# Attention of a two-layer fp32 trunk in 24 sections of fixed TensorE order, its value sums divided in place of its weights, with a 512-wide output product

## The chip, the cores and the metric

The kernel runs on one core of one Trainium2 chip. The metric is device time in microseconds of one execution, taken as the median of several runs. TensorE (PE in the profile), VectorE (DVE), ScalarE (ACT), GpSimd (POOL) and SyncE (SP, which here issues DMAs) each take their own instructions in a fixed order and wait for each other by semaphores.

## The reference

Two layers on 640 tokens of width 1024: one block of 128 context tokens (`xp`) and four of 128 latent tokens (`xs`), all in fp32. Layer 0 has grouped-query attention (8 heads of 64, 2 key heads) beside a depthwise convolution of 31 taps on 512 channels; both go into one output product. Layer 1 is an mLSTM. Each layer ends with a squared-ReLU feed-forward part, and every sub-layer is modulated by vectors from a conditioning product (`_adaln`), six vectors of 1024 a layer.

```python
m = jax.nn.silu(cond) @ w + b          # six modulation vectors a layer
h = x * (1 + scale) + shift
q, k, v, u = jnp.split(h @ w_in, [...])
s = jnp.einsum('bqkgd,bskd->bkgqs', q_r, k_all) * scale   # context: 128 keys; latent: 640 keys
p = jax.nn.softmax(s, axis=-1)
att = jnp.einsum('bkgqs,bskd->bqkgd', p, v_all)
u = a * jax.nn.sigmoid(gt)
u = jax.nn.silu(_layernorm(_depthwise_conv(u, conv_w, conv_b), cln_g, cln_b))
out = jnp.concatenate([att, u], axis=-1) @ w_out          # (640 x 1024) @ (1024 x 1024)
x = _layernorm(ALPHA * x + gate * out, g, b)
x = _layernorm(ALPHA * x + gate2 * (relu(modulate(x) @ w1) ** 2 @ w2), g2, b2)
```

## The kernel before, in words

Large products are made of fp32 numbers split into a rounded high part and a low rest; `mm3` (lines 192 to 195) issues three matmuls for one: high by high, high by low, low by high. Weights come by DMA into a `raw` tile, ScalarE casts the high part `whi` (L166) and GpSimd subtracts the low part `wlo` (L167), both into a ring of slots (`split_piece`).

The program is written in one order, and a scheduler places each instruction in its engine's queue by priorities and estimated times. On the chip each queue then runs as it stands.

Attention (line 1118 on) works on four pairs of heads. `prep(i)` makes the q of a pair: for each token block a cast (L1135) and a subtraction on DVE (L1136) give high and low part, two transposes (L1139) and a copy (L1141) bring them to PE's layout. `weights_of` makes scores with matmuls (L1172 for context, L1186 for a latent block and head, 640 keys) and calls `softmax`: maximum on DVE (L1151), exponential on ScalarE (L1153, it also gives the row sum), reciprocal on DVE (L1154), and the division of the whole row of weights on DVE (L1156, 128 x 640). `values_of` turns the weights with transposes (L1218), copies them out of PSUM (L1221 on ScalarE for key block 0, L1223 on DVE for the others), and multiplies by the values (L1225), key block by key block, into `po`. `put_att` splits the sums into `act_h` and `act_l` (L1160, L1161).

The modulation vectors come from `ada_steps` (L259): the 1024 x 1024 part of `w_ada` is streamed in eight k-tiles (two DMAs of 256 KB each, L287, into slots of the weight ring) and multiplied with 32 columns of the array at a time (L293). `background(n)` issues one such step of each waiting vector; seven vectors are computed during the attention.

`conv(i)` sums the 31 taps of channel block i in one tile `cy`, in one chain: some taps on DVE (L955, L964), the others as a product on ScalarE (L969, tile `tap`, two buffers) and an add on GpSimd (L971). `CONV_DVE` says which taps go to DVE. `conv_norm` (L1254 to L1294) makes the layer norm and the swish; it is called after the ninth of twelve units of the attention.

`out_proj` (L455) makes the 640 x 1024 output product in four groups of 256 columns, each with eight k-tiles at once (0 to 3 attention channels, 4 to 7 conv channels) for the five token blocks; `add_gated` multiplies by the gate and adds to the residual, and `finish` starts the layer norm of a token block. The feed-forward part of layer 0 follows.

## Time and profile before

| | before |
|---|---|
| median of 3 runs | 1731.96 us (1729.14 to 1732.87) |
| profiled execution | 1730.38 us |
| its span, first to last instruction | 1728.4 us |
| mean granted clock of TensorE | 0.971 |
| PE busy | 1603.1 us (93%) |
| DVE busy | 1098.2 us (64%) |
| POOL busy | 1005.0 us (58%) |
| ACT busy | 797.0 us (46%) |
| moved by DMA | 211.76 MB, 123 GB/s |

Busy time is the union of an engine's instructions. PE's matmuls overlap in the records: a duration is longer than the distance from one start to the next, so the pace of PE is read from starts. A fp32 matmul (a modulation step, a value block) leaves two records, a matmul of split parts one. In the rows below, "idle before" is the time an engine stood still ahead of an instruction, and the name after the arrow is what ended it.

### The profile page before, as it was taken

The numbers are of one execution on the slowest core, as the hardware profiler recorded it, in microseconds if no ns is written. First come the engines' busy times: TensorE is split into PE (matmuls) and PEld (weight loads), VectorE is DVE, ScalarE is ACT, GpSimd is POOL, SyncE is SP. The second block draws the span as 40 slices with busy tenths as digits, with TensorE's granted clock in tenths as the row PEclk, the third lists the DMA queues.
The fourth block names the chain that finished last, engine by engine and source line by source line (L and its number), as shares of the span: only waits on it lengthen the run. The fifth ranks groups of instructions, "written<-read, shape, count | busy, mean of one in ns | idle before, by whom it ended". The sixth has DMA issues, their size and how long they took to land. (4 is left out here: it accounts for less than half of the span.)

```text
span 1728.4 us, 27385 instructions
## 1 busy us (share of the span) xinstructions
PE 1603.1 (93%) x10155; PEld 1408.6 (81%) x10155; DVE 1098.2 (64%) x1924; ACT 797.0 (46%) x1560; POOL 1005.0 (58%) x760
## 2 busy tenths in 40 slices
PE   7988899998989999999898998997989999999996
PEld 4678555897879889897798998896988989989885
DVE  2899997669434354356777787688497254344367
ACT  2224676345444444444544555555265444344344
POOL 2245574147956556457655766756459755546555
PEclk9999899998989999999999999998999999999998
DMA  8852785223433223125232222326442422213241
GB/s 302 250 192 82 256 310 189 62 93 122 135 91 98 70 78 98 60 87 185 90 109 81 88 66 93 113 83 201 117 159 79 128 93 92 94 53 98 86 152 68
DMA packets 151309, 211.76 MB, mean 123 GB/s; under 512 B 11845, under 2 KB 92969, under 8 KB 151176
## 3 DMA queue, kind: packets, MB, share of 16 engines
q1 hardware_dynamic: 150944, 209.94, 37.8%
q8 instruction: 80, 1.31, 0.3%
q14 instruction: 53, 0.43, 0.1%
q10 hardware_dynamic: 232, 0.08, 0.0%
HBM read 186.74 MB, written 23.24 MB: 121 GB/s over the span
## 5 line engine op out<-in xcount | busy, mean ns | idle before, releaser
L167 POOL TENSOR_TENSOR wlo<-raw,whi 128x512 fp32r<-128x512 f32 x370 | 512.8, 1408 | 405.6 <-ACT whi L166 391.5
L166 ACT CAST whi<-raw 128x512 fp32r<-128x512 f32 x364 | 222.4, 620 | 427.6 <-PE ps L195 194.3
L193 PE MATMUL ps<-whi,h 128*128 128x512 f32 x640 | 254.4, 399 | 13.7 <-DVE pr L526 6.9
L194 PE MATMUL ps<-wlo,h 128*128 128x512 f32 x640 | 254.8, 398 | 0.0
L195 PE MATMUL ps<-whi,h 128*128 128x512 f32 x640 | 254.3, 397 | 0.0
L193 PE MATMUL ps<-act_h,whi 128*128 128x320 f32 (+2 forms) x704 | 221.9, 317 | 7.2 <-ACT act_h L625 5.9
L194 PE MATMUL ps<-act_l,whi 128*128 128x320 f32 (+2 forms) x704 | 221.6, 315 | 4.2 <-POOL act_l L626 2.2
L195 PE MATMUL ps<-act_h,wlo 128*128 128x320 f32 (+2 forms) x704 | 221.0, 315 | 2.3 <-POOL wlo L167 2.3
L167 POOL TENSOR_TENSOR wlo<-s,whi 128x512 fp32r<-128x512 f32 x118 | 162.8, 1383 | 73.8 <-ACT whi L166 61.3
L758 DVE TENSOR_TENSOR acc<-acc,ps 128x512 f32<-128x512 f32 x120 | 81.9, 685 | 161.6 <-PE ps L195 161.6
L193 PEld LDWEIGHTS ps<-whi,h 128*128 128x128 f32 x640 | 121.7, 190 | 42.8 <-DVE pr L526 7.1
L193 PEld LDWEIGHTS ps<-act_h,whi 128*128 128x128 f32 x704 | 135.7, 193 | 12.3 <-ACT act_h L625 6.7
L195 PEld LDWEIGHTS ps<-whi,h 128*128 128x128 f32 x640 | 121.4, 190 | 29.2
L194 PEld LDWEIGHTS ps<-wlo,h 128*128 128x128 f32 x640 | 121.6, 190 | 27.3
L194 PEld LDWEIGHTS ps<-act_l,whi 128*128 128x128 f32 x704 | 135.6, 193 | 7.3 <-DVE act_l L626 2.8
L195 PEld LDWEIGHTS ps<-act_h,wlo 128*128 128x128 f32 x704 | 135.6, 193 | 3.1 <-POOL wlo L167 3.1
L193 PE MATMUL ps<-whi,act_h 128*128 128x256 f32 x440 | 125.7, 289 | 1.1 <-DVE acc L1094 1.1
L194 PE MATMUL ps<-wlo,act_h 128*128 128x256 f32 x440 | 124.4, 286 | 0.0
L195 PE MATMUL ps<-whi,act_l 128*128 128x256 f32 x440 | 123.3, 286 | 0.0
L971 POOL TENSOR_TENSOR cy<-cy,tap 128x655 f32<-128x655 f32 x50 | 80.4, 1607 | 53.8 <-DVE cy L964 22.5
L193 PE MATMUL ps<-T_h,whi 128*128 128x320 f32 x336 | 104.0, 310 | 4.0 <-ACT pr L550 2.8
L166 ACT CAST whi<-s 128x512 fp32r<-128x512 f32 x120 | 73.2, 616 | 68.9 <-DVE s L501 52.6
(440 smaller groups left out, 4064.1 us busy)
## 6 DMA issues: line engine op xcount, KB each, us to landing
raw<-in_w_ff_dram SPq DMA_DIRECT2D x128, 512.0 KB
whi<-in_w_ada_dram SPq DMA_DIRECT2D x80, 256.0 KB
wlo<-in_w_ada_dram SPq DMA_DIRECT2D x80, 256.0 KB
raw<-in_w_in_m_dram SPq DMA_DIRECT2D x32, 512.0 KB
ada_w<-in_w_ada_dram SPq DMA_DIRECT2D x32, 256.0 KB
acc_d<-acc SPq DMA_DIRECT2D x15, 512.0 KB
raw<-in_w_in_a_dram SPq DMA_DIRECT2D x12, 512.0 KB
rx<-acc_d SPq DMA_DIRECT2D x20, 256.0 KB
```

What stands on the lines that cost most here:

```text
L166: nc.scalar.copy(out=hv, in_=src)
L167: (eng or nc.gpsimd).tensor_tensor(out=lv, in0=src, in1=f32(hv), op=ALU.subtract)
L193: nc.tensor.matmul(out=out, lhsT=lh, rhs=rh, start=start, stop=False)
L194: nc.tensor.matmul(out=out, lhsT=lh, rhs=rl, start=False, stop=False)
L195: nc.tensor.matmul(out=out, lhsT=ll, rhs=rh, start=False, stop=stop)
L758: nc.vector.tensor_tensor(out=x, in0=x, in1=ps, op=ALU.add)
L971: nc.gpsimd.tensor_tensor(out=y, in0=y, in1=tp, op=ALU.add)
```

## The change

- The conv's last channel block takes every third tap on DVE (11) in place of every eighth (4).
- While the attention is written, each PE instruction is tied to the one before it (`in_turn`), so that PE's order is the written one.
- The attention is written as 24 sections, three for each half of a pair of heads: two key blocks turned and copied, scores of later blocks between them, one call for modulation (two k-tiles, `ada_group = 2`, in the first 20 sections), then the values of both blocks; the third section has one key block and the context block or the divisors.
- `prep` makes one cast and one subtraction for all five token blocks (128 x 640 each), and yields between its transposes.
- Weights of latent blocks stay undivided. The row sums of a pair's eight blocks stand in one tile; their reciprocals are spread to 128 x 512, turned by four transposes, and the value sums are multiplied by them (`latent_out`). Context weights are divided on ScalarE.
- Key block 4 instead of block 0 is copied by ScalarE.
- Five modulation vectors instead of seven are computed in the attention; the last two go to the feed-forward part of layer 0.
- x is loaded again and scaled before the last three sections, and `conv_norm` is written after the attention.
- `out_proj_halves` takes 512 columns at a time. The first half runs over the five token blocks twice: k-tiles 0 to 3 (attention), then 4 to 7 (conv), in five PSUM banks. Four of the second half's weight pieces use other tiles than the ring.

```diff
-CONV_DVE = (range(31), range(31), range(0, 31, 4), range(0, 31, 8))
-PT_ACT = (0,)
+CONV_DVE = (range(31), range(31), range(0, 31, 4), range(0, 31, 3))
+PT_ACT = (4,)
-ADA_IN_ATT = 7
+ADA_IN_ATT = 5
+ADA_PAIRS = 20
+    def in_turn(ins):
+        if K.ordered:
+            if K.pe is not None:
+                tc.add_manual_dep(
+                    ins, K.pe.name, mybir.DependencyInfo(mybir.DependencyClass.NoSync, mybir.DependencyReason.DATA),
+                    reason="order of the attention")
+            K.pe = ins
...
-            if k:
+            if k and k % K.ada_group == 0:
                 yield
...
+    def out_proj_halves(w, S, finish):
+        ah, al = act
+        ws = load_n512(w, 0)
+        pss = [ps1() for _ in range(NT)]
+        for k0 in (0, 4):
+            for t in range(NT):
+                sl = slice(t * P, (t + 1) * P)
+                for k in range(k0, k0 + 4):
+                    mm3(pss[t], ah[:, k, sl], al[:, k, sl], *ws[k], k == 0, k == KT - 1)
+                if k0:
+                    add_gated(pss[t], t, S.gate, 0, 512, S.tmp)
...
+        for t in range(NT):
+            ps = ps1()
+            tm_tile(ws, act, t, ps)
+            add_gated(ps, t, S.gate, 512, 512, S.tmp, nc.vector)
+            finish(t)
...
+            qs = att.tile([P, NT, 2, P], F32R, name="qs", bufs=1)
+            nc.scalar.copy(out=qs[:, :, :, 0:64], in_=q)
+            nc.vector.tensor_tensor(out=qs[:, :, :, 64:128], in0=q, in1=f32(qs[:, :, :, 0:64]), op=ALU.subtract)
...
-            nc.vector.reciprocal(out=ri, in_=sm)
-            d2 = dst.rearrange("p a b -> p (a b)") if multi else dst
-            nc.vector.tensor_scalar(out=d2, in0=d2, scalar1=ri[:, 0:1], scalar2=None, op0=ALU.mult)
...
+        def divisors(i):
+            ri = att.tile([P, 8], F32, name="ri8")
+            nc.vector.reciprocal(out=ri, in_=sums[i])
+            rb = rawp.tile([P, 1024], F32, name="raw")
+            nc.vector.tensor_copy(
+                out=rb[:, 0:512].rearrange("p (o d) -> p o d", d=HD), in_=ri.unsqueeze(2).broadcast_to([P, 8, HD]))
+            return rb
+        def divisors_turned(rb):
+            tp = ps1()
+            for t in range(4):
+                transpose(out=tp[:, t * P:(t + 1) * P], in_=rb[:, t * P:(t + 1) * P], identity=ident)
+            nc.scalar.copy(out=rb[:, 512:1024], in_=tp)
+        def latent_out(i, rb):
+            x, sl = rb[:, 512:1024], slice(P, TOK)
+            nc.vector.tensor_tensor(out=x, in0=POs[i], in1=x, op=ALU.mult)
+            nc.scalar.copy(out=act[0][:, i, sl], in_=x)
+            nc.vector.tensor_tensor(out=act[1][:, i, sl], in0=x, in1=f32(act[0][:, i, sl]), op=ALU.subtract)
...
+                p0 = turned(i, s, 0)
+                next_weights()
+                p1 = turned(i, s, 1)
+                if s == 0:
+                    next(parts, None)
+                elif i + 1 < pairs:
+                    context_weights(i + 1)
+                modulation()
+                values(i, s, 0, p0)
+                values(i, s, 1, p1)
...
-        out_proj(I["w_out_a"][0], S, S.finish_mixer("f0"))
+        out_proj_halves(I["w_out_a"][0], S, S.finish_mixer("f0"))
```

The first place is DVE's queue in the middle of the attention. `cy` is the chain of conv taps, `ptok` a row of weights, `nm` a maximum, `ri` a reciprocal. Before:

```order
L1136 TENSOR_TENSOR qs<-acc,qs 128x2x64
L1156 TENSOR_SCALAR ptok<-ptok,ri 128x640
L1151 TENSOR_REDUCE nm<-ps_2779 128x1
L1136 TENSOR_TENSOR qs<-acc,qs 128x2x64
L964 SCALAR_TENSOR_TENSOR cy<-up,cw,cy 128x655
L1154 RECIPROCAL ri<-sm 128x1
L1156 TENSOR_SCALAR ptok<-ptok,ri 128x640
L1151 TENSOR_REDUCE nm<-ps_2910 128x1
```

Now, in the seventh and eighth section (L1251 is the copy of turned weights, L1016 the tap, L1203 the maximum):

```order
L1016 SCALAR_TENSOR_TENSOR cy<-up,cw,cy 128x655
L1251 COPY pT<-ps_2565 128x512
L1016 SCALAR_TENSOR_TENSOR cy<-up,cw,cy 128x655
L1203 TENSOR_REDUCE nm<-ps_2572 128x1
L1251 COPY pT<-ps_2581 128x512
L1285 RECIPROCAL ri_2787<-sums 128x8
L1287 COPY raw<-ri_2787 128x512
L1185 TENSOR_TENSOR qs<-acc,qs 128x10x64
L1203 TENSOR_REDUCE nm<-ps_2631 128x1
L1016 SCALAR_TENSOR_TENSOR cy<-up,cw,cy 128x655
L1203 TENSOR_REDUCE nm<-ps_2640 128x1
```

The divisions of `ptok` and their reciprocals are gone, the five subtractions of q are one, and taps of the conv chain stand between the copies and maxima of neighbouring sections.

The second place is PE's queue in the attention, between the turning of one pair of key blocks and the next (`psc` is a sum of modulation steps, `po` the value sums). Before:

```order
L1218 MATMUL ps1_2445<-ident_75,ptok_2299 128x128
L293 MATMUL psc_2512<-wlo_2562,stat_109 32x256 x2
L1186 MATMUL ps2_2582<-kTA_503,qT_2223 128x320
L1186 MATMUL ps2_2582<-kTB_504,qT_2223 128x320
L293 MATMUL psc_2512<-whi_2631,stat_109 32x256 x2
L293 MATMUL psc_2512<-wlo_2632,stat_109 32x256 x2
L1225 MATMUL po_2307<-pT_2349,vS_505 64x256 x2
L1218 MATMUL ps1_2454<-ident_75,ptok_2260 128x128
```

Now, the end of a third section and the start of the next:

```order
L127 MATMUL ps2_2456<-kTA_503,qT_2112 128x320
L127 MATMUL ps2_2456<-kTB_504,qT_2112 128x320
L127 MATMUL psc_2362<-whi_2465,stat_109 32x256 x2
L127 MATMUL psc_2362<-wlo_2466,stat_109 32x256 x2
L127 MATMUL psc_2362<-whi_2473,stat_109 32x256 x2
L127 MATMUL psc_2362<-wlo_2474,stat_109 32x256 x2
L127 MATMUL po_2184<-pT_2435,vS_505 64x256 x2
L130 MATMUL ps1_2486<-ident_75,ptok_2260 128x128
```

Half k-tiles that stood among scores have become a run of two whole k-tiles, straight ahead of the values.

The third place is PE's queue in the feed-forward part, where a group of first products (`act_h`, 320 wide) and of second products (`h`, 512 wide) meet. Before:

```order
L195 MATMUL ps_5045<-act_h,wlo 128x320
L193 MATMUL ps_5088<-whi,h 128x512
L194 MATMUL ps_5088<-wlo,h 128x512
L195 MATMUL ps_5088<-whi,h 128x512
```

Now, at one such meeting:

```order
L214 MATMUL ps_4602<-wlo,h 128x512
L215 MATMUL ps_4602<-whi,h 128x512
L127 MATMUL psc<-whi,stat 32x256 x2
L127 MATMUL psc<-wlo,stat 32x256 x2
L213 MATMUL ps_4677<-act_h,whi 128x320
L214 MATMUL ps_4677<-act_l,whi 128x320
L215 MATMUL ps_4677<-act_h,wlo 128x320
```

The k-tiles of the two moved vectors stand in seven groups of one to three between the products.

## Rows read from the trace of the kernel before

**Rows 1.** The page's engine line: busy us, share of the span, instructions.

```profile
PE 1603.1 (93%) x10155; PEld 1408.6 (81%) x10155; DVE 1098.2 (64%) x1924; ACT 797.0 (46%) x1560; POOL 1005.0 (58%) x760
```

**Rows 2.** Stretches: length, busy of PE, PEld, DVE, ACT, POOL, clock, DMA share, GB/s.

```profile
183.00:326.00 143.00, 132.28 (x1012) 76.23 (x1009) 123.07 (x254) 86.96 (x181) 68.39 (x48) 0.95 0.62 215
...
240.00:260.00 20.00, 18.96 (x173) 10.31 (x169) 18.59 (x40) 15.02 (x33) 13.37 (x10) 1.00 1.01 373
...
498.00:505.00 7.00, 0.12 (x2) 0.10 (x1) 1.76 (x3) 2.25 (x4) 3.58 (x3) 0.65 0.48 167
540.00:800.00 260.00, 260.00 (x1430) 233.66 (x1429) 116.39 (x181) 110.20 (x180) 146.50 (x111) 1.00 0.28 88
```

**Rows 3.** Timeline of PE: start us, us, engine, line, operation, tiles, count.

```profile
180.62 0.39 PE L293 MATMUL psc<-whi,stat 128*32 128x256 f32 x2
...
182.56 0.39 PE L293 MATMUL psc<-whi,stat 128*32 128x256 f32 x2
...
217.43 0.66 PE L1218 MATMUL ps<-ident,ptok 128*128 128x128 f32 x4
...
218.02 0.41 PE L293 MATMUL psc<-whi,stat 128*32 128x256 f32 x2
...
218.59 0.41 PE L1186 MATMUL ps<-kTA,qT 128*128 128x320 f32 x1
...
224.93 0.65 PE L1225 MATMUL po<-pT,vS 128*64 128x256 f32 x4
225.51 0.66 PE L1218 MATMUL ps<-ident,ptok 128*128 128x128 f32 x4
225.93 0.39 PE L1186 MATMUL ps<-kTA,qT 128*128 128x320 f32 x1
...
226.68 0.44 PE L1225 MATMUL po<-pT,vS 128*64 128x256 f32 x2
...
445.23 0.39 PE L193 MATMUL ps<-whi,h 128*128 128x512 f32 x1
...
459.15 0.31 PE L193 MATMUL ps<-act_h,whi 128*128 128x320 f32 x1
```

**Rows 4.** DVE's groups by shape, 183 to 327 us: busy, mean ns, idle before.

```profile
L1156 DVE TENSOR_SCALAR ptok<-ptok,ri 128x640 f32<-128x640 f32 x32 | 28.7, 896 | 0.5
...
L1136 DVE TENSOR_TENSOR qs<-acc,qs 128x128 fp32r<-128x128 f32 x18 | 10.5, 586 | 0.0
...
L964 DVE SCALAR_TENSOR_TENSOR cy<-up,cw,cy 128x655 f32<-128x655 f32 x6 | 5.3, 890 | 0.0
L1156 DVE TENSOR_SCALAR pp<-pp,ri 128x128 f32<-128x128 f32 x8 | 5.3, 662 | 0.1
```

**Rows 5.** Timeline of DVE: a division of weights.

```profile
212.19 1.91 DVE L1156 TENSOR_SCALAR ptok<-ptok,ri 128x640 f32<-128x640 f32 x1
```

**Rows 6.** Timeline of POOL: two taps of the conv.

```profile
212.17 1.58 POOL L971 TENSOR_TENSOR cy<-cy,tap 128x655 f32<-128x655 f32 x1 [1.52 <-ACT tap L969]
...
267.74 1.57 POOL L971 TENSOR_TENSOR cy<-cy,tap 128x655 f32<-128x655 f32 x1 [0.18 <-ACT tap L969]
```

**Rows 7.** POOL's groups by shape, 132 to 327 us.

```profile
L971 POOL TENSOR_TENSOR cy<-cy,tap 128x655 f32<-128x655 f32 x50 | 80.4, 1607 | 53.8 <-DVE cy L964 22.5 <-ACT tap L969 10.3 <-DVE ri L1154 8.7
```

**Rows 8.** PE's groups by shape, 183 to 327 us: half of the modulation steps.

```profile
L293 PE MATMUL psc<-wlo,stat 128*32 128x256 f32 x203 | 31.7, 412 | 0.0
```

**Rows 9.** ACT's groups by shape, 183 to 327 us.

```profile
L969 ACT ACTIVATE tap<-up,cw 128x655 f32<-128x655 f32 x33 | 27.6, 840 | 13.1 <-POOL cy L971 13.1
```

**Rows 10.** PE's groups by shape, 326 to 386 us: the output product.

```profile
L193 PE MATMUL ps<-whi,act_h 128*128 128x256 f32 x160 | 44.7, 284 | 0.0
```

**Rows 11.** PE's groups by shape, 445.2 to 459.2 us: 512 columns.

```profile
L194 PE MATMUL ps<-wlo,h 128*128 128x512 f32 x20 | 7.9, 395 | 0.0
```

**Rows 12.** Timeline of PE behind the output product.

```profile
407.51 1.01 PE L193 MATMUL ps<-act_h,whi 128*128 128x384 f32 x2 [5.00 <-ACT act_h L625]
```

**Rows 13.** Waits, 480 to 520 us: us in total, times, longest.

```profile
ACT whi L166 <- DMA raw<-in_w_ff_dram: 14.4, 3, 12.4
```

More of the change, by code (lines that the diff above doesn't have):

```diff
@@ new lines, in context_weights @@
+        def context_weights(i):
+            qT, g = qTs[i], i // 2
+            sp = ps2()
+            pp = Ps[i, -1] = att.tile([P, 2, P], F32, name="pp")
+            for h in range(2):
+                for x, kT in enumerate((kTA, kTB)):
+                    matmul(
+                        out=sp[:, h, 0:P], lhsT=qT[:, h, 0:P], rhs=kT[:, g, 0:P], start=(x == 0), stop=(x == 1))
+            for h in range(2):
+                sm = att.tile([P, 1], F32, name="smc")
+                exps(sp[:, h, 0:P], pp[:, h, :], sm, False)
+                ri = att.tile([P, 1], F32, name="ri")
+                nc.vector.reciprocal(out=ri, in_=sm)
+                nc.scalar.activation(out=pp[:, h, :], in_=pp[:, h, :], func=AF.Copy, scale=ri[:, 0:1])
@@ new lines, in turned @@
+        def turned(i, s, j):
+            tp = ps1()
+            for h in range(2):
+                for t in range(2):
+                    o = (h * 2 + t) * P
+                    transpose(
+                        out=tp[:, o:o + P], in_=Ps[i, 1 + 2 * s + t, h][:, j * P:(j + 1) * P], identity=ident)
+            pT = att.tile([P, DEC], F32, name="pT", bufs=2)
+            if j in PT_ACT:
+                nc.scalar.copy(out=pT, in_=tp)
+            else:
+                nc.vector.tensor_copy(out=pT, in_=tp)
+            return pT
@@ new lines, in context_values @@
+        def context_values(i, pT):
+            vg = slice((i // 2) * HD, (i // 2 + 1) * HD)
+            po = ps1()
+            for h in range(2):
+                matmul(
+                    out=po[64 * h:64 * h + 64, 0:P], lhsT=vS[:, 0, vg], rhs=pT[:, h * P:(h + 1) * P],
+                    start=True, stop=True, tile_position=(0, 64 * h))
+            nc.scalar.copy(out=act[0][:, i, 0:P], in_=po[:, 0:P])
+            nc.vector.tensor_tensor(
+                out=act[1][:, i, 0:P], in0=po[:, 0:P], in1=f32(act[0][:, i, 0:P]), op=ALU.subtract)
@@ new lines, in trunk_kernel, with next_weights, modulation @@
+        K.ordered = True
+        pairs = HEADS // 2
+        jobs = [(i, t, h) for i in range(pairs) for t in range(1, NT) for h in range(2)]
+        def next_weights(n=1):
+            for _ in range(n):
+                if jobs:
+                    latent_weights(*jobs.pop(0))
+        section = 0
+        def modulation():
+            nonlocal section
+            if section < ADA_PAIRS:
+                background(1)
+            section += 1
+        for _ in prep(0):
+            pass
```

209 lines of the change are left out of this document (107 added, 102 removed).

## The prediction

> **What bounds the kernel now.** I read the page's engine line first, then busy time by stretches, then the groups of the attention, and last the timeline of TensorE (PE), which gives the spacing of instructions that their durations don't. Of the profiled span of 1728.4 us PE is busy for 1603.1, 93% [rows 1]. So in each stage the question is whether the change leaves PE less to issue, or lets it wait less. The attention runs from 183 to 326 us; VectorE (DVE) is busy for 123 of these 143 us and PE for 132; in the middle, 240 to 260, DVE has 18.6 and PE 19.0 of 20 [rows 2]. So neither can be emptied there without the other setting the pace. The feed-forward part is PE alone, 260.0 of 260 us from 540 to 800 [rows 2], and so is the output product (326 to 386). What is taken from DVE in the attention is worth something; what is added to PE in the feed-forward part costs its full length.
>
> In the timeline I read from one start to the next [rows 3]. Four transposes take 0.42 us when scores follow (225.51 to 225.93) and 0.59 when narrow matmuls of 32 columns of the array follow (217.43 to 218.02): a change of form costs about 0.15. One k-tile of a modulation vector (eight records) on its own takes 0.57 (218.02 to 218.59), in an unbroken run 0.43 (180.62 to 182.56 is nine half k-tiles of 0.215). Four scores with the change are 0.75 (225.93 to 226.68), so 0.60 without. One value block is 0.58 (224.93 to 225.51).
>
> **The change, part by part.**
>
> *Work taken off DVE in the attention.* The 32 divisions of weights are 28.7 us, those of the context weights 5.3 [rows 4]; 40 reciprocals shrink to 12. Larger and fewer subtractions of q (some 7 us less of the 10.5 of L1136) stand against 7 more taps of 0.89 (6.2) and four products of a divisor with a value sum (0.68 each, as the copies of that size). DVE loses about 33 of its 123 us. One division takes 1.91 us where a GpSimd tap has just started (212.17 and 212.19 [rows 5, 6]), against a mean of 0.90; so part of the mean is waiting for GpSimd, and I count the whole of it as gone. By the Trainium skill, SBUF — State Buffer (SBUF: two separate sides), DVE and GpSimd hold one port pair in turn and the loser blocks for a whole instruction; so GpSimd's adds should shorten too when the divisions go. The rows leave little for that: an add takes 1.57 or 1.58 here and 1.61 in the mean [rows 6, 7].
>
> *PE in the attention.* Seven vectors become five, in 20 sections of two k-tiles. Two k-tiles in a run are 2 x 0.43 + 0.15 = 1.0, so 20 us; before, the 405 records in this stretch, half of them in [rows 8], stood in pieces, many of half a k-tile, and summed over the pieces' spacing they take 39 us, with 4 of waiting. Value blocks in pairs: 0.43 + 0.43 + 0.15 = 1.0 for two, against 1.16. Four transposes of divisors for each of four head pairs are new (0.6 each, 2.3 in all). A section with two blocks is then 0.42 + 0.60 + 0.59 + 0.45 (q transposes or context scores) + 1.0 + 1.0 = 4.06, the third of a half about 3.9. The last 16 sections come to 5.33 x 12.0 = 64, less four without a modulation pair (4), six without a score group (4) and about 2 where no q transposes are left, plus the PE work of the conv's norm (10.7 us, summed from the spacing of its records), which the order puts among them: about 65. All 24 by the same count: 98.
>
> *The wait that takes the divisions' place.* The conv's last channel block now has a DVE tap at every third place. Each interval is two GpSimd adds of 1.61 [rows 7], one DVE tap of 0.89 [rows 4] and two handovers, 0.26 together (an estimate from the shortest wait shown for a tap, 0.18 [rows 6]): 4.35. Ten such DVE taps stand in DVE's order between the copies of sections one to eight, so the copies behind each wait for the chain, and PE, itself in fixed order, for the copies. Before, the first weight transposes started at 209; I leave the start at 208, since the q preparation ahead of it still waits for the rotated q. Nine intervals are 39 us: section nine starts at 247, where PE alone would be at 241. ScalarE's taps also stand ahead of exponentials in its queue; it waited 13.1 us for GpSimd in this way [rows 9], and DVE's wait covers that.
>
> So the attention ends at 247 + 65 + 2 (small waits, an estimate from the releasers of its idle time, each under 1 us) = 314 instead of 326: **minus 12**. Bounds: minus 20 (PE alone: 208 + 98) and 0 (the chain gives back everything).
>
> *Output product.* 480 matmuls of 256 columns become 240 of 512. The durations, 283 and 395 ns [rows 10, 11], would shrink the product by 30 per cent, 17 us. The spacing says otherwise: 480 in 57.4 us (60 less the other work of 326 to 386) is 0.120 each; sixty of 512 columns take 445.23 to 459.15, 0.232 each [rows 3]. So 57.4 becomes 55.7. The conv's channels come second, so PE starts without them, but the norm is now last in program order: I add 2 to 3 us of waiting at the second pass (none to 5). The last token tile's layer norm, behind which PE waits 5.0 [rows 12], no longer has weight casts among its work on DVE: minus 2 (0 to minus 4). Sum **minus 1** (minus 6 to plus 4). The Trainium skill, TensorE: Matmul & The Clock Gate (Back-to-back issue gap), gives N/2.4 + 2.5 ns for an isolated matmul, near the rows at both widths, but 131 ns as the sustained figure at 512 columns. By that figure 240 would be an estimated 31 us, 24 below my term; the measured 0.232 is against it.
>
> *Two vectors moved to the feed-forward part.* 16 k-tiles in seven groups between its matmuls, with two changes of form each: 16 x 0.43 + 14 x 0.15 = **plus 9**. Bounds: 18 if every half k-tile costs the 0.57 of a whole one alone [rows 3]; 2 if most of them fill the 6.9 us hole at 498 to 505 [rows 2], where PE waits for weights that arrive late (ScalarE waits 14.4 us for the transfers [rows 13]). Into SP's queue just there go 32 loads of 256 KB more, past the feed-forward weights, so I expect no filling, rather up to 4 us more; I take 9. The same 8 MB leave the attention, where the transfers were once at their ceiling (share 1.01 from 240 to 260 [rows 2]); since PE had 18.96 there, that gives at most 1 us, inside the bounds.
>
> The pool closed early, and x reloaded before the last three sections, are hidden by those sections; late, x would hold only the residual. Nothing.
>
> Sum: -12 - 1 + 9 = -4, on the profiled execution's own 1730.4: 1726.4. That lies 1.6 below the median of the runs (1731.96), which would make it 1728; I give 1727.5. A measurement of this kernel can tell about 0.2% (3.5 us) from no change, so the forecast is just inside faster.
>
> **Rivals.**
>
> 1. *The chain doesn't bind.* GpSimd, with no divisions beside it, adds at 1.57, DVE takes each tap on time, and PE runs from 208 to 306. For it: DVE is left with 90 us of work in 118. Against: ten taps at fixed places. Attention minus 20, total minus 12: 1719.
> 2. *Slower: a ring holds the attention, and the moved vectors are paid in full.* In sections one to eight each DVE tap waits for two GpSimd adds, these for ScalarE's taps, these for the exponentials ahead of them, these for scores, which in PE's fixed order stand behind matmuls that wait for the copies behind the DVE tap. It decides from an interval of 5.6 us instead of 4.35 (nine of them eat the 12). For it: GpSimd waited 10.3 us for ScalarE's taps and, from 132 us on, 22.5 for DVE's [rows 7]. Then attention 0, product 0 to +2, feed-forward +9 to +13: 1739 to 1745.
> 3. *The moved vectors fill the hole.* They cost 2: 1721.
> 4. *Width pays per instruction, as the durations say.* 17 us more off: 1711. The skill's sustained figure, named above, would put this at 1704.
> 5. *Nothing moves.* PE is at 19.0 of 20 in the middle already; the fixed order repeats what the scheduler found, and what is gained pays the 9: 1732.
>
> **How the numbers follow.** Forecast 0.40 (its own range 1720 to 1735, from the product's bounds and half of the chain's), rival 1 0.23, rival 2 0.22, rival 3 0.08, rival 4 0.02, rival 5 0.05. The range goes down to 1706 (rival 1 with the product's and the hole's lower bounds in part) and up to 1743 in rival 2. Faster by over 0.2% (under 1728.5): half of the forecast and rivals 1, 3 and 4, 0.54. Same: a third of the forecast and rival 5, 0.20. Slower (over 1735.4): rival 2 and the forecast's upper end, 0.26.
>
> **What would show it.** Attention: transposes of section nine near 247, DVE idle ahead of its conv taps (releaser GpSimd) before that, PE at 19.5 of 20 after it, first output matmul near 314. Under 308 is rival 1, 322 or later rival 2. Product: a spacing of 0.232 and a wait of PE at the second pass. Feed-forward: seven groups of narrow matmuls, 9 us together, the hole no shorter. The forecast is wrong if the attention's end moves by less than 6 or more than 18 us, or if the time from the product's end to the end of the first feed-forward part grows by less than 4 or more than 14.

## The result and the profile after

The changed kernel takes 1740.7 us (median of 12 runs, 1735.12 to 1750.4) against 1732.41 for the kernel before on the same chip (12 runs): ratio 1.0051, 95% interval 1.0032 to 1.0069. It is slower by half a per cent; the forecast was 0.26% faster. The profiled span is 1737.0 us at a granted clock of 0.961 (before: 1728.4 at 0.971). The engine line, to be held against [rows 1]:

```profile
PE 1595.8 (92%) x9931; PEld 1406.0 (81%) x9931; DVE 1073.6 (62%) x1840; ACT 796.2 (46%) x1549; POOL 990.2 (57%) x748
```

PE has 7 us less work, DVE 25 less, and the span is 9 longer. So the time is in PE's waits and in its clock, not in work that was added. I cut the span at PE's starts (first and last matmul of the output product, first 384-wide matmul of the feed-forward part, its last product, first `psi` product of layer 1); the rest runs to the end of PE's last matmul, some 14 us before the span's end. Lengths in us; two experiments told of below stand beside them:

| stage | before | after | wide product alone (e16) | all but the wide product (e18) |
|---|---|---|---|---|
| start to first output matmul | 326.0 | 324.6 | 324.4 | 324.5 |
| output product | 59.9 | 68.6 | 57.1 | 68.3 |
| from there to the feed-forward part | 21.6 | 19.4 | 19.3 | 21.7 |
| feed-forward part | 437.5 | 440.6 | 431.7 | 445.9 |
| to layer 1's first product | 44.0 | 45.2 | 44.9 | 45.2 |
| rest | 825.0 | 824.3 | 827.7 | 828.0 |

The old attention in e16 also ends 1.6 earlier (and in e14 and e17, told of below, 1.2 and 2.3 later), so the 1.4 that the new attention gains is no more than the same code varies.

The stretches of after (columns as in [rows 2]):

```profile
240.00:260.00 20.00, 18.87 (x174) 11.84 (x169) 13.82 (x32) 12.71 (x26) 6.82 (x6) 0.92 0.84 296
284.00:303.00 19.00, 18.72 (x134) 14.60 (x130) 12.80 (x23) 10.08 (x22) 0.67 (x1) 1.00 0.10 30
303.00:325.00 22.00, 16.18 (x88) 11.26 (x87) 13.29 (x27) 5.41 (x11) 9.56 (x9) 0.61 0.24 84
...
498.00:505.00 7.00, 6.32 (x44) 5.79 (x43) 0.57 (x2) 1.40 (x4) 4.08 (x4) 1.00 0.72 234
540.00:800.00 260.00, 260.00 (x1423) 233.10 (x1422) 118.10 (x181) 109.67 (x179) 143.08 (x110) 1.00 0.25 80
```

DVE was emptied as forecast (13.8 of 20 in the middle, 18.6 before), yet PE is no busier there. The bad stretch is the attention's end, 303 to 325: 5.8 us idle, and a mean clock of 0.61 between the levels of 1.2 and 2.4 GHz. Before, the same stretch reads:

```profile
303.00:325.00 22.00, 21.44 (x150) 15.21 (x149) 16.70 (x45) 7.12 (x15) 0.00 (x0) 0.92 0.00 1
```

The one engine that is new there is GpSimd: 9.56 us busy against 0.00. The norm itself is not new there: though it was written earlier, the kernel before ran it at the same time, its one-column matmuls from 302 to 309 us and the small operations of its inverse square root from 309 to 315, each in 0.15 to 0.17 us:

```profile
309.41 0.17 DVE L396 TENSOR_SCALAR rc<-rh_v 128x5 int32<-128x5 int32 x1
309.62 0.17 DVE L397 TENSOR_SCALAR rc<-rc 128x5 int32<-128x5 int32 x1
```

The timeline of DVE in after shows what GpSimd does to them (128x5, three operations and then three rounds of four; start us, us, engine, line):

```profile
307.39 0.17 DVE L416 TENSOR_SCALAR rc<-rh_v 128x5 int32<-128x5 int32 x1
307.60 1.28 DVE L417 TENSOR_SCALAR rc<-rc 128x5 int32<-128x5 int32 x1
308.91 1.19 DVE L420 TENSOR_TENSOR rh_a<-rc 128x5 f32<-128x5 f32 x1
310.13 1.19 DVE L421 TENSOR_TENSOR rh_a<-rh_a,rh_v 128x5 f32<-128x5 f32 x1
311.35 1.19 DVE L422 TENSOR_SCALAR rh_a<-rh_a 128x5 f32<-128x5 f32 x1
312.58 0.17 DVE L423 TENSOR_TENSOR rc<-rh_a,rc 128x5 f32<-128x5 f32 x1
...
313.47 0.68 DVE L1251 COPY pT<-ps 128x512 f32<-128x512 f32 x1
...
315.62 1.20 DVE L422 TENSOR_SCALAR rh_a<-rh_a 128x5 f32<-128x5 f32 x1
...
316.93 0.69 DVE L1251 COPY pT<-ps 128x512 f32<-128x512 f32 x1
```

and GpSimd's, which splits the output product's weights at that time:

```profile
307.58 4.93 POOL L187 TENSOR_TENSOR wlo<-raw,whi 128x512 fp32r<-128x512 f32 x4 [2.75 <-ACT whi L186]
314.30 2.48 POOL L187 TENSOR_TENSOR wlo<-raw,whi 128x512 fp32r<-128x512 f32 x2 [1.79 <-ACT whi L186]
```

A split takes 1.23 us (4.93 for four), and an operation of 0.17 us that meets one takes 1.13 to 1.28 (six of the fifteen do). The copies of turned weights (L1251) stand behind them in DVE's queue, and PE, in its fixed order, behind the copies:

```profile
300.22 2.29 PE L1340 MATMUL psc<-ones,csq 128*128 128x1 f32 x20
303.02 1.28 PE L1340 MATMUL psc<-ones,csq 128*128 128x1 f32 x10
...
314.21 1.12 PE L130 MATMUL ps<-ident,ptok 128*128 128x128 f32 x4 [4.53 <-DVE pT L1251]
317.67 0.69 PE L127 MATMUL po<-pT,vS 128*64 128x256 f32 x2 [1.29 <-DVE pT L1251]
```

Ahead of the low clock PE ran the norm's one-column matmuls (L1340). So it did before, and the clock fell there too, to 0.66 between 308 and 313; but PE had work all that time, and from 313 on the clock was 1.00. In after it stayed at half (0.50 from 304.5 to 320.5), with PE busy for 10.2 of these 16 us. In the output product the gate vector is what comes late. Timeline of SP's queue, then of DVE, then of PE, in after:

```profile
324.38 1.08 SPq L297 DMA_DIRECT2D ada_m<-in_b_ada_dram  x2
328.54 16.01 SPq L169 DMA_DIRECT2D raw<-in_w_out_a_dram  x2
344.61 1.02 SPq L353 DMA_DIRECT2D h<-gate_d  x2
```

```profile
353.70 0.69 DVE L471 TENSOR_TENSOR s<-ps,h 128x512 f32<-128x512 f32 x1 [10.69 <-DMA h<-gate_d]
361.38 0.69 DVE L471 TENSOR_TENSOR s<-ps,h 128x512 f32<-128x512 f32 x1 [7.00 <-DMA h<-gate_d]
```

```profile
354.44 0.50 PE L213 MATMUL ps<-whi,act_h 128*128 128x512 f32 x1 [1.76 <-DVE s L471]
354.78 0.39 PE L214 MATMUL ps<-wlo,act_h 128*128 128x512 f32 x1
355.01 0.39 PE L215 MATMUL ps<-whi,act_l 128*128 128x512 f32 x1
...
362.13 0.50 PE L213 MATMUL ps<-whi,act_h 128*128 128x512 f32 x1 [1.83 <-DVE s L471]
...
363.17 0.63 PE L213 MATMUL ps<-whi,act_h 128*128 128x512 f32 x1
363.60 0.63 PE L214 MATMUL ps<-wlo,act_h 128*128 128x512 f32 x1
...
384.83 0.66 PE L713 MATMUL ps_t<-ident,acc 128*128 128x128 f32 x4 [2.92 <-ACT h L381]
```

The gate's loads stand behind weight loads of the second half, whose issue was stuck for 16 us; before, they were issued at 325.56. The longest wait of SP there, 15.2 us, is for a GpSimd split; the split waits for its cast on ScalarE, which runs at 337.05; and the cast waits for PE, which in two passes needs the ring slot of the first k-tile until its last token block has used it, at 336.96. GpSimd's timeline:

```profile
337.75 8.92 POOL L187 TENSOR_TENSOR wlo<-raw,whi 128x512 fp32r<-128x512 f32 x4 [14.37 <-ACT whi L186]
```

After PE's first wait the spacing is 0.23 as ahead of it (354.78 to 355.01); after the second it is 0.43 (363.17 to 363.60), at a granted clock of 0.50.

### The profile page after: what moved, and what is told of

It reads as the page before. It is cut to its first block, busy times and chain, and to the rows that moved or that the text cites. A ratio compares the mean times of both kernels' runs of the same rounds, so it can differ in the third digit from the quotient of the medians.

```text
span 1737.0 us, 26768 instructions
## 1 busy us (share of the span) xinstructions
PE 1595.8 (92%) x9931; PEld 1406.0 (81%) x9931; DVE 1073.6 (62%) x1840; ACT 796.2 (46%) x1549; POOL 990.2 (57%) x748
## 3 DMA queue, kind: packets, MB, share of 16 engines
q8 instruction: 78, 1.28, 0.3%
## 5 line engine op out<-in xcount | busy, mean ns | idle before, releaser
L213 PE MATMUL ps<-whi,act_h 128*128 128x256 f32 (+1 forms) x340 | 106.0, 314 | 4.2 <-DVE s L471 3.6
L214 PE MATMUL ps<-wlo,act_h 128*128 128x256 f32 (+1 forms) x340 | 104.9, 310 | 0.0
L214 PE MATMUL ps<-T_l,whi 128*128 128x320 f32 x336 | 104.0, 309 | 0.0
L215 PE MATMUL ps<-T_h,wlo 128*128 128x320 f32 x336 | 103.9, 309 | 0.0
```

What stands on the lines that cost most here:

```text
L213: nc.tensor.matmul(out=out, lhsT=lh, rhs=rh, start=start, stop=False)
L214: nc.tensor.matmul(out=out, lhsT=lh, rhs=rl, start=False, stop=False)
L215: nc.tensor.matmul(out=out, lhsT=ll, rhs=rh, start=False, stop=stop)
```

## The experiments

All are edits of the changed kernel unless another is named, and each ratio is to the kernel before on the same chip. Theory A says that the loss sits in these waits (the splits beside the norm, the late gate); its rivals put it elsewhere: in the conv chain, in the norm's place, in the number of vectors, or in the fixed order. Where an expectation defines its letters otherwise, its own words hold.

**e1: the gate first.** The second half's loads are ordered behind the gate's.

```diff
-            nc.sync.dma_start(
+            K.gate_dma = nc.sync.dma_start(
                 out=gt[:, c, :].rearrange("p (j n) -> p j n", j=4),
...
-        nc.sync.dma_start(out=v, in_=src)
+        d = nc.sync.dma_start(out=v, in_=src).ins
+        if K.behind is not None:
+            tc.add_manual_dep(d, K.behind.name, ..., reason="gate first")
...
+        K.behind = K.gate_dma
         ws = load_n512(w, 512, {
...
+        K.behind = None
```

> The changed kernel, with the two loads of the gate put ahead of the four weight loads of the output product's second half in SP's queue (order only, no new wait). Theory A (two places lose the time: the last four attention sections and the late gate): the gate lands by about 335, the waits of PE at 354 and 362 us (1.8 each) go, the adds of the first half are done 10 to 15 us earlier, and the product from its first to its last matmul falls from 69 us by 4 to 6; total 1735 to 1737 against 1740.7. Rival B (the product is longer because of the two passes and the conv channels coming second, not because of the gate): the gate lands early and the product stays at 66 to 69 us; total within 2 us of the changed kernel. Rival C (the moved modulation vectors make the loss): no change either.

Measured: 1744.89, ratio 1.0081 [1.0057, 1.0104]. The product fell from 68.6 to 55.6 us, PE has no idle time in it and its clock is 1.00 (0.95 in after): the late gate does cost the product what it seems to, and more than twice what theory A expected. But the layer norm behind it took 27.7 instead of 19.4, so that both together fall by 4.6 only (88.0 to 83.3), and the feed-forward part took 450.1 instead of 440.6; the waits that are new there are at a group of the moved vectors' k-tiles, which came late (3.58, 2.19 and 1.00 us). The stage is explained, the total not improved.

**e5: the splits after the norm.** The first half's splits wait for the last operation of the inverse root.

```diff
-            nc.vector.tensor_tensor(out=out, in0=a, in1=out, op=ALU.mult)
+            K.rs = nc.vector.tensor_tensor(out=out, in0=a, in1=out, op=ALU.mult).ins
...
+        if K.after is not None:
+            tc.add_manual_dep(lo_ins, K.after.name, ..., reason="split late")
...
+        K.after = K.rs
         ws = load_n512(w, 0)
+        K.after = None
```

> The changed kernel, with one wait added: GpSimd's first split of the output product's weights waits for the last of the norm's 13 small DVE operations. Measures the collision by itself. Theory A: the small operations that took 1.2 us take 0.17 (six of them, 6 us in all), PE's wait of 4.5 us at 310 goes, the first output matmul comes 4 to 6 us earlier (319 to 321), if the splits, now 5 us later, are still done by then; total 3 to 6 us less. Rival B (the small operations are slow for another reason, such as what they wait for on PE): they stay at 1.2 us and the product starts later by the delay of the splits, total 0 to 5 us more.

Measured: 1749.46, ratio 1.0107 [1.0086, 1.0128]. The attention's end moved from 324.6 to 319.7. In its DVE timeline the small operations are back at 0.17, and the 4.53 us wait of PE is gone:

```profile
307.40 0.17 DVE L423 TENSOR_SCALAR rc<-rc 128x5 int32<-128x5 int32 x1
307.61 0.17 DVE L426 TENSOR_TENSOR rh_a<-rc 128x5 f32<-128x5 f32 x1
307.81 0.17 DVE L427 TENSOR_TENSOR rh_a<-rh_a,rh_v 128x5 f32<-128x5 f32 x1
```

So the splits cost the attention 4.9 us: shown. The total is worse all the same, because the feed-forward part grew to 454.4; the waits of that part name the moved vectors' loads:

```profile
PE psc L129 <- DMA whi<-in_w_ada_dram: 8.3, 2, 7.4
```

**e12: no norm.** The conv's layer norm and swish are left out; the conv's sums are only split into high and low parts.

```diff
         def conv_norm():
-            ones = cl.tile([P, P], F32, name="ones")
...
+            for i in range(4):
+                for c0, n, o in ((0, P, 0), (PAD + P, DEC, P)):
+                    hi, lo = (x[:, 4 + i, o:o + n] for x in act)
+                    nc.scalar.copy(out=hi, in_=cy[:, i, c0:c0 + n])
+                    CN_LO[i % 2].tensor_tensor(out=lo, in0=cy[:, i, c0:c0 + n], in1=f32(hi), op=ALU.subtract)
```

> The changed kernel without the conv's layer norm and swish: means, squares, the 13 small DVE operations, the spread sums and the activation are left out, and the convolution's sums are only split into the two parts that the output product takes. Measures what the norm costs where it stands. Theory A (the forecast's count of the last sections was right, and the norm's chain on DVE makes the rest): PE's own norm work of 10.7 us and the waits both go, the first output matmul comes at 301 to 306, 19 to 23 us before the changed kernel's 324.6. Rival B (PE or the copies set the last sections anyway): only the 10.7 go, 313 to 315.

Measured (one execution): 1729.94 beside 1732.12; first output matmul at 313.7, 10.9 earlier, which is rival B's figure. Its last eight sections take 23.7 us against 40.8 in after: 17 less, of which the norm's own matmuls are 10.7 (the prediction's count) and about 6 the waits and low clock of 303 to 325. Its earlier sections ran 6.3 later for no reason that the edit gives, so the split of the 10.9 is only rough, and it does not by itself decide against rival B.

**e13: the conv chain.** Every eighth tap on DVE, as before.

```diff
-CONV_DVE = (range(31), range(31), range(0, 31, 4), range(0, 31, 3))
+CONV_DVE = (range(31), range(31), range(0, 31, 4), range(0, 31, 8))
```

> The changed kernel with the conv's last channel block as before, every eighth tap on DVE. The forecast had these taps set the pace of sections one to eight (section nine at 247; it came at 247.6). If they do: with four DVE taps instead of eleven, copies wait less, section nine starts at 241 to 244 and the attention ends 3 to 6 us earlier. If they don't (DVE waited only 3.2 us for the chain in the changed kernel, the half clock until 211 and the ends of the vectors make the rest): section nine stays at 246 to 249, total within 2 us of the changed kernel.

Measured: 1742.78, ratio 1.0066 [1.0048, 1.0084]; first output matmul 325.1 instead of 324.6. With 4 of 11 DVE taps the attention is as long. The chain does not set its pace.

**e2 and e6: the norm earlier.** `conv_norm` is written before the fifth of eight half pairs (e2), and the same with e1's edit (e6).

```diff
+                if (i, s) == (2, 0):
+                    ups.close()
+                    cl = cls.enter_context(tc.tile_pool(name="cl", bufs=1, side="right", reuse_waits="tile"))
+                    conv_norm()
```

> The changed kernel, with the conv's norm written behind the first half of the third pair of heads and no longer behind the whole attention. Theory A (the norm's chain of 13 small DVE operations stands ahead of the copies of the last sections, waits for PE's one-column sums and collides with GpSimd's weight splits, and PE in fixed order stands still and falls to half clock): the small operations are back at 0.17 us, PE has no wait over 1 us after 290, the first matmul of the output product comes at 310 to 316 instead of 324.6; total 8 to 12 us less, 1729 to 1733. Rival B (PE alone sets the pace of the last sections): the norm's work only changes place, the first output matmul stays at 322 to 326. Rival C (an earlier norm makes the earlier sections wait instead): the sections at 260 to 285 get longer by what the last ones gain.

> Both edits together: gate ahead of the second half's weights, and the conv's norm written behind the first half of the third pair of heads. Theory A: the two losses are in different places and add up: first output matmul at 310 to 316, product 63 to 65 us; total 1724 to 1729, under the kernel before (1732.4). Rival B (what is won ahead of the feed-forward part is given back there, where weights arrive late): the stages are earlier as said, but the wait for weights behind them grows by as much, total 1732 to 1737.

Measured: 1.0139 [1.0119, 1.0160] and 1.0133 [1.0109, 1.0156]; first output matmul at 341.5 and 340.5. Theory A and rival B of e2 and both theories of e6 missed; rival C of e2 has the direction, not the size. An earlier norm does not help but costs 16 to 17 us: PE's norm matmuls then run as a block from 284 to 312, with waits up to 3.50 us between them, ahead of the sections that are tied to each other. The gate, though, is not late in e2: its loads are issued at 340.63, before the first output matmul, as they are in e12 (312.78) and in e11 below (321.62), and DVE does not wait for them. The divisors use a raw slot there as well, so these alone do not make the gate late: what counts is whether the scheduler puts the gate's loads ahead of the second half's weights or behind them. Nor is the gate all that can lengthen the product: in e2 and e12 it takes 63.3 us with one wait, of 3.25 and 3.46 us, for the layer norm of a token block.

**e11: no tie.** The attention as written, but PE's order left to the scheduler.

```diff
-        K.ordered = True
+        K.ordered = False
```

> The changed kernel without the ties between PE's instructions: the sections are written in the same order, the scheduler is free to move them. Theory A (in the last sections PE stands still because the written order keeps it behind copies that wait for the norm): the scheduler puts scores and values where the norm's matmuls now leave PE waiting, the first output matmul comes 3 to 8 us earlier (317 to 322). Rival F (the fixed order is what makes sections nine to twenty run at 4 us each): these sections get longer, first output matmul at 328 or later, total 1744 or more.

Measured: 1761.07, ratio 1.0176 [1.0147, 1.0206]; first output matmul at 327.4, 2.8 later, the product 9.5 shorter, but 13 us more in the feed-forward part and 11 in layer 1, where nothing was edited. Neither theory came out whole. The attention's end is not held back by the tie.

**e8, e7, e15: more vectors in the attention.** Seven in 24 sections (e8), the same with e1's edit (e7); six in 24 sections with e1's edit (e15).

```diff
-ADA_IN_ATT = 5
-ADA_PAIRS = 20
+ADA_IN_ATT = 7
+ADA_PAIRS = 24
...
-        K.ada_group = 2
+        K.ada_group = 3
```

> The changed kernel with all seven vectors in the attention (three k-tiles in each of 21 sections), and nothing else. Theory A with D: attention 4 to 7 us longer, feed-forward part 3 us shorter (441 to 438, the hole of 7 us of the kernel before comes back), start of the second layer as in the changed kernel; total 1 to 4 us more than the changed kernel's 1740.7. Rival C (the moved vectors are the main loss): attention unchanged because the extra k-tiles fill waits there, total 1731 to 1734, as the kernel before.

> The changed kernel with the gate loads ahead of the second half's weights, and with all seven modulation vectors in the attention (three k-tiles in each of 21 sections), none in the feed-forward part. With the gate edit alone the product fell to 56 us, but the feed-forward part grew to 450 us with PE waiting for late k-tiles of the moved vectors. Theory D (those k-tiles, behind the gate loads in SP's queue, make the feed-forward part long): it is back at 436 to 439 us; the attention grows by 16 x 0.43 = 7 us or less; sum 3 to 8 us under the kernel with the gate edit alone (1744.9), 1737 to 1742. Rival E (the feed-forward part is bound by its own weights' transfers, and whatever arrives early waits there): it stays at 446 to 452, total 1748 to 1753.

> The changed kernel with the gate loads ahead of the second half's weights and a sixth modulation vector in the last four sections of the attention, so that one is left for the feed-forward part. Theory D: PE stands still for some 9 us in those sections, so the eight k-tiles (4 us of PE) lengthen the attention by 0 to 4; the feed-forward part falls from 450 to 438 to 443 us as fewer k-tiles come late; total 1734 to 1740. Rival: with k-tiles among them the last sections grow as they did with seven vectors (0.9 us for each k-tile, 7 us), total 1741 to 1745.

Measured: e8 1746.05, ratio 1.0082 [1.0056, 1.0107]; e7 1741.62, 1.0062 [1.0040, 1.0083]; e15 1760.52, 1.0167 [1.0152, 1.0182]. With seven vectors the attention ends at 339.4 (e8), 14.8 later than with five, where 4 to 7 were expected, and 13 later than the old one with as many; the feed-forward part is 431.3, so the two moved vectors cost 440.6 - 431.3 = 9.3 there. With the gate first it is 450.1 - 431.7 = 18.4. e7's total lies in theory D's 1737 to 1742 by luck: its attention is 16.9 longer than e1's, not 7 or less, and its feed-forward part is shorter than expected. In e15 the attention ends 4.9 earlier than in after although it has a vector more, and the product takes 66.5 us with the gate first, since it now waits for the conv's channels (2.31 and 4.47 us); both expectations failed. It also lost 15 us in layer 1, where nothing was edited, so its total tells nothing on the vectors.

**e4: before, with five vectors.** The edit is `ADA_IN_ATT = 5` in the kernel before.

> The kernel before with one part of the change alone: two of the seven vectors moved from the attention to the feed-forward part. By the spacing read before, the attention has 16 k-tiles less at 0.6 to 0.8 (10 to 13 us less PE work), of which its second full engine, VectorE, lets through 0 to 6; the feed-forward part takes 9 us of PE, less up to 7 if they fill its hole, plus what PE waits for late k-tiles. Theory D: total 0 to 8 us more than before (1732 to 1740). Rival C': the attention gives back the whole 10, total 1724 to 1729.

Measured: 1736.3, ratio 1.0031 [1.0016, 1.0046]. The attention ends at 321.3, 4.7 earlier; the feed-forward part is 6.8 longer, the stretch from it to layer 1 2.9 longer, and layer 1 starts 5.0 later. So moving two vectors is a loss in the old kernel too, and with five vectors the old attention ends 3.3 before the new one.

**e14, e16, e17: before, with the wide product.** e16 puts `load_n512` and `out_proj_halves` into the kernel before and nothing else; e14 adds e1's edit, and e17 is e14 again.

```diff
-        out_proj(I["w_out_a"][0], S, S.finish_mixer("f0"))
+        out_proj_halves(I["w_out_a"][0], S, S.finish_mixer("f0"))
```

> The kernel before with the 512-wide output product in two passes alone, its gate loads ahead of the second half's weights. By spacing the product falls from 57.4 to 55.7 us of matmuls, and it can start without the conv channels. In the changed kernel with the same gate order it took 55.6 from first to last matmul, and the tail behind it 27.7 instead of 21.6. Theory A (the tail, a chain of VectorE and ScalarE for each token block, takes what the product gives): from first output matmul to feed-forward part 80 to 84 us against 81.5; total 1728 to 1735, no change. Rival G (the tail in the changed kernel was long for another reason): 76 to 78 us, total 1726 to 1729.

> The kernel before with the 512-wide output product alone: old attention with seven vectors, no tie between gate loads and the second half's weights. Theory A (the gate loads stand behind the second half's weight loads in SP's queue, whatever the attention): from the first output matmul to the first 384-wide product of the feed-forward part 86 to 90 us as in the changed kernel (88.0), the feed-forward part 428 to 433 us as in e14 (the hole at 505 us gone by the width alone), ratio to the kernel before 1.001 to 1.004. Rival B (the gate was late in the changed kernel only because the divisors use the raw slots and the norm comes last): 79 to 83 us, ratio 0.996 to 0.999. Rival C (the hole goes by the gate tie of e14 and not by the width): feed-forward part 436 to 439 us.

> The kernel of e14 once more, in five more rounds (old attention, 512-wide product, gate loads ahead of the second half's weights). Theory A (what e14 showed is a gain of about 0.13 per cent): ratio 0.9975 to 0.9995 with an interval below 1.0. Rival B (no difference): 0.9995 to 1.001.

Measured: e14 0.9987 [0.9972, 1.0002], e17 0.9993 [0.9978, 1.0008], no difference to be told; e16 **1722.97 us, 0.9960 [0.9945, 0.9975]**, faster than both kernels. The product takes 57.1 us, and the gate is not late without any tie, as SP's queue in e16 shows:

```profile
323.99 0.98 SPq L334 DMA_DIRECT2D h<-gate_d  x2
335.25 0.37 SPq L150 DMA_DIRECT2D raw<-in_w_out_a_dram  x1
```

From the product's start to the feed-forward part it is 76.4 us, under the 79 to 83 of rival B (whose ratio came) and far from the 86 to 90 of theory A: the width alone does not make the gate late. The cast that holds the loads up in after runs at 336.60 here, no earlier; but the gate's loads stand ahead of it in SP's queue. With the new attention alone (e18, below) they stand behind, and DVE waits 3.10 us for them; the 10.69 and 7.00 of after come with both. The feed-forward part is 431.7: the hole of [rows 2] goes by the width alone, the first 512-wide product there waiting 1.76 us instead of 6.88. Before, then e16:

```profile
504.91 0.80 PE L193 MATMUL ps<-whi,h 128*128 128x512 f32 x1 [6.88 <-DVE pr L526]
...
493.84 0.50 PE L194 MATMUL ps<-whi,h 128*128 128x512 f32 x1 [1.76 <-DVE pr L558]
```

e14 and e17 differ from e16 by the tie of the loads only, and take 24 us in place of 19.3 from the product to the feed-forward part. Their attention, where the edit is not, also ends 2.8 and 3.9 later, so how much of the difference of 6 to 7 us the tie makes itself stays open.

**e18: the new attention with the old product.** The line above, turned round, in the changed kernel.

> The changed kernel with the old output product of 256-wide groups: the new attention alone. Theory A (the attention gains 1 us, the moved vectors cost 9 in the feed-forward part and nothing fills the hole at 505 us, since only the wide product does): first output matmul at 324 to 328 us, output product plus tail 81 to 85 us, feed-forward part 444 to 449 us, with the hole (a wait of 5 to 8 us near 505); ratio 1.003 to 1.007. Rival B (the moved vectors' k-tiles fill the hole): feed-forward part 437 to 441 us, hole under 2 us, ratio 0.999 to 1.002. Rival C (without 512 columns the norm at the end is not hidden, since the first group needs the conv's channels): product plus tail over 90 us, ratio above 1.008.

Measured: 1747.85, ratio 1.0102 [1.0085, 1.0118]. The feed-forward part is as theory A has it (445.9), but without a hole: 3.9 us of small waits between 485 and 496 in its place, as rival B has it. Product and what follows take 90.0 us and the ratio is above 1.008, which is rival C's forecast: the product is 68.3 us, since the conv's channels, now last, are waited for:

```profile
334.87 0.39 PE L213 MATMUL ps<-whi,act_h 128*128 128x256 f32 x1 [2.70 <-ACT act_h L1365]
...
336.22 0.41 PE L213 MATMUL ps<-whi,act_h 128*128 128x256 f32 x1
336.44 0.41 PE L214 MATMUL ps<-wlo,act_h 128*128 128x256 f32 x1
...
342.63 0.28 PE L215 MATMUL ps<-whi,act_l 128*128 128x256 f32 x1
342.76 0.28 PE L213 MATMUL ps<-whi,act_h 128*128 128x256 f32 x1
```

After the wait the spacing is 0.21 for 7 us where it is 0.12 later.

In total the two halves of the change add up: e16 is 8.4 us below the kernel before (1722.97 against 1731.36 on that chip), e18 16.5 above; together +8.1, and the change measured +8.3. By stages they do not. Up to layer 1's first product the table has minus 11.6 for e16 and plus 16.6 for e18, together plus 5.0, and plus 9.3 for the change; the rest, where nothing was edited, is 2.7 longer in e16, 3.0 longer in e18 and 0.7 shorter in after. So the sign of each half is shown, and the close sum is partly luck.

## Why the prediction was wrong

The sign was wrong, the time just inside the range (1706 to 1743). Both of its signs of being wrong came: the attention's end moved by 1.4 us (less than 6), and the time from the product's end to the end of the first feed-forward part grew by 0.8 (less than 4). By its steps:

- **Start 208, section nine at 247: right in the numbers** (206.8 and 247.64), wrong in the reason. The step "nine intervals of 4.35 us of the conv chain" fell: DVE waited for GpSimd in its taps only 3.2 us in all (five times, longest 2.2), and e13 takes most taps away without effect. What held PE there were a clock of 0.93 and 3.9 us of waiting in 207 to 247 (36.12 us busy of 40), of which the ends of modulation vectors are the largest pieces (the rows are of 200 to 284; 2.4 and 0.8 of them lie in 207 to 247):

```profile
PE psc L130 <- DVE ada_m L317: 3.5, 3, 2.4
PE psc L127 <- DVE ada_m L317: 1.5, 2, 0.8
```

- **"65 + 2 small waits": the step that failed most.** The last 16 sections took 77 us, not 67, and the attention ended at 324.6, not 314: minus 1.4 for minus 12. The count of PE's work was good: 98 us alone, and 117.8 measured (206.8 to 324.6) less 12.4 of idle time (five stretches from 207 to 325) leaves 105; the 7 above 98 I put down to the stretches at a low clock, 0.61 in the last 22 us; that is not tried by itself. What I left out is what the weight splits of the next stage do beside the norm; e5 shows 4.9 us of it. The other half of the ten us was not isolated. The prediction had cited the Trainium skill, SBUF — State Buffer (SBUF: two separate sides), for the lock that DVE and GpSimd share, but only where it would help. The same rule spoke against the change: the loser blocks for the whole instruction, and the rows agree, 0.17 becoming 1.13 to 1.28 beside splits of 1.23. What I drew from it, shorter adds on GpSimd, did not come: 1.60 us in the mean against 1.61. DVE's busy time in 183 to 326 fell by 27 us, not 33.

- **A cover that the sum did not see.** Before, the scheduler put modulation steps (82 records, ten k-tiles) into the attention's start, where PE waits for the rotated q. Now its order has none there, and PE waits 12.7 us for the subtraction of q (L1185). Before, then after:

```profile
183.00:207.00 24.00, 18.72 (x137) 10.12 (x134) 21.57 (x42) 14.46 (x33) 10.50 (x8) 0.79 0.83 288
...
183.00:207.00 24.00, 10.58 (x39) 8.75 (x40) 17.11 (x22) 16.45 (x31) 15.26 (x10) 0.50 0.00 1
```

  PE does 8 us less there and must do it later. I had kept the start but not asked what filled it. That this is why five vectors cost the new attention as much as seven the old was not tried by itself.

- **Output product: the width right, its wait wrong.** The spacing of 0.232 held (0.23 in the rows above), and the width alone gives minus 2.8 in e16, for my minus 1.7. The durations' 17 us (rival 4) did not come, nor the sustained 131 ns that the prediction named from the Trainium skill, TensorE: Matmul & The Clock Gate (Back-to-back issue gap). The step "2 to 3 us at the second pass (none to 5)" named the wrong wait: the second pass hid the norm, with no wait there, but the gate came late, 6.5 us of waits in the rows above (1.76, 1.83, 2.92) and spells at half clock after two of them; with the gate first (e1) all of it is gone. The product was 68.6, plus 8.7; from there to the feed-forward part minus 2.3, near the forecast (minus 2). In SP's queue I had counted the loads that the change adds to the feed-forward part and not those that it puts ahead of the gate. The second half's loads wait for raw slots, and these for splits whose casts wait for the ring slots of the first pass (15.2 us); the divisors, which use the raw tile too, hold a load up for 3.0 us there.

- **Two moved vectors, plus 9: right.** Seven groups, together 9.15 us, and 9.3 as the difference of e8. But the feed-forward part grew by 3.1 only, because the wide product took the hole away (minus 5.8 in e16), which the prediction held fixed. "The hole no shorter" is wrong for the vectors too: with them and the old product (e4, e18) the wait of 6.88 us is gone as well, the longest in its place 1.69 and 1.86. Yet the part is 6.8 and 8.4 longer than before there, so rival 3's cost of 2 is wrong, and its figure came near by another cause.

- **Layer 1's start** (plus 1.2) was not forecast. Before, PE waits 4.60 + 0.55 us there; in after and in e16 alike 1.17 and 5.8:

```profile
857.55 0.66 PE L395 MATMUL ps<-ident,acc 128*128 128x128 f32 x4 [1.17 <-DVE act_l L402]
...
864.01 0.58 PE L213 MATMUL psc<-h,act_h 128*128 128x256 f32 x1 [5.80 <-ACT act_h L401]
```

  The two waits go with the wide product, but the length does not: e18 has 45.2 with the old one (waits of 5.67 and 0.55). Why stays open.

- **Rivals.** Rival 1 fell with the attention's end, though its claim that the chain does not bind was the right one. Rival 2 gave the right time (1739 to 1745) by a mechanism, the ring through DVE's taps, that e13 refutes. Rival 5's attention (PE already full) is near what happened in time, not in cause: PE stood idle for 12.4 us. Two sums of the working are slightly off: the interval of the conv chain adds up to 4.37, not 4.35, and the shares of the forecast and the rivals to chances of 0.53, 0.18 and 0.29, not 0.54, 0.20 and 0.26.

## What to carry to other kernels

Freeing an engine at a stage's bound pays only if the stage's other limits stay where they were: ask of each hole in the old schedule what filled it, and of each engine that becomes idle what the scheduler will move there. When a step is written last, list everything that now runs beside it (here the next product's weight splits on GpSimd, beside which DVE's small operations took 1.2 us for 0.17) and everything that now stands ahead of its consumers in the DMA queue. A change of two parts should be timed in halves: here one half wins 8 us and the other loses 16. Compare the halves by stages too: equal sums can hide parts that do not add.

## What the runs showed of the hardware

- DVE operations on 128x5 took 1.13 to 1.28 us in place of 0.17 beside GpSimd splits of 1.23 us, although five numbers a partition are moved; without the splits they are back at 0.17 (e5), as they are in the kernel before.
- After a wait of 1.83 us that came 8 us behind one of 1.76, 512-column matmuls ran at a spacing of 0.43 instead of 0.23 for 3 us (362.75 to 365.73 in after, granted clock 0.50); after the 1.76 itself the clock stayed at 1.00. In e18, 256-column ones ran at 0.21 instead of 0.12 for 7 us after a wait of 2.70, with waits of 0.77 and 0.35 among them (clock 0.52). So a wait of this size can cost more than its length, and need not.
- In the stretch behind some 30 one-column matmuls the clock was 0.61 with PE busy 16 of 22 us; with the splits away (e5), PE was busy 20 of 22 and the clock 0.77. Before, with as many of them and PE busy 21.4 of 22, it was 0.92; without the norm (e12) it was 1.00 from 290 to the attention's end, with PE busy 21 of 24.
